# A two-layer hybrid generator on one core: the latent's GDN solution moved beside its RWKV scan, 84 instead of 64 expert slots placed first, and latent projections ahead of the context's later queries

## The chip, the cores and the metric

The kernel runs on 1 core of one Trainium2 chip. The metric is the device time of one execution in microseconds (us), lower is better. Three executions of the kernel before took 3139.51, 3136.21 and 3149.08 us, a median of 3139.51 us.

## The reference, cut to what matters

There are two layers over 256 latent tokens and 256 context tokens, width 1024, float32. Layer 0 mixes each stream by two bidirectional recurrences side by side (a chunked gated DeltaNet, "GDN", and RWKV-7), projects out, and runs PEER, a product-key expert layer. The latent stream starts from the final recurrence states of the context. Layer 1 needs the context only as keys and values of its attention.

```python
def even_layer(x_ctx, x_lat, ...):
    y_ctx, ctx_states = even_mixer(pre(x_ctx, ...) @ w_in, zeros, **mix)
    y_lat, _ = even_mixer(pre(x_lat, ...) @ w_in, ctx_states, **mix)
    x_lat = ffn_residual(x_lat + ml[2] * (y_lat @ w_out), ...)   # PEER
    x_ctx = ffn_residual(x_ctx + mc[2] * (y_ctx @ w_out), ...)   # PEER

def gdn_chunk_scan(q, k, v, g, beta, s0):          # chunks of 64
    lower = I + strict_lower((k*beta) @ k.T * decay)
    u, w = solve_triangular(lower, [v*beta, k*beta*exp(G)])
    # then 4 steps over the chunks, each needing the state of the last

def peer(h, wq, k1, k2, u, v):
    # per token, 8 heads: top 16 of 128 keys, twice; top 16 of the 256 pairs
    act = gelu(sum(u[eid] * h)); out = sum(gate * act * v[eid])
```

PEER reads, for each token, 8 x 16 rows of u and of v at computed indices.

## The kernel before, in words

**Slots.** A PEER tile is 128 tokens. Its 128 (head, rank) pairs are 128 slots of `experts` (L1263). A slot gathers one 2048-wide row of `peer_uv` per token (1 MB) by an indirect DMA that POOL issues (L1278), forms the dot product on DVE (L1281), the gelu and a diagonal matrix `di` on ACT and DVE (L1287 to L1291), and adds the v row into two PSUM banks by two 128x512 matmuls (L1293). Six buffers `g8` hold gathered rows, so about six gathers run ahead. There are six tiles: context 1 and 2, latent 1 and 2 in layer 0, and two in layer 1, 768 slots in all. Context tile 2 is cut: its first `CUT` = 64 slots (L152, L1785) stand directly behind context tile 1, the other 64 stand in layer 1 (L1806), beside the Hyena convolution.

**Picks.** Before a slot can be gathered its indices must be known. `peer_prep` (L1109) runs queries and scores for two heads at a time; `pick` (L1229) finds the top 16 on DVE, and its last row (L1253) writes the indices `ei` that the gathers of 32 slots read. The scores of tile 2 are kept and picked after those of tile 1.

**The latent mixer.** `rwkv_prep` (L721) projects and builds blocks, `solve` (L586) inverts triangular blocks (30 pairs of DVE operations in `solve1`, with a trip through DRAM ahead, `dn`, and one behind, `yd`, L619 and L632 to L634), `gdn_prep` (L428) projects q, k, v, and then computes the decays and the blocks N; `rwkv_scan` (L867) has four steps, `gates` (L959) four projections, `gdn_scan` (L664) four steps. Then come `rwkv_out`, `gdn_out`, `out_proj` and the latent's `peer_prep`.

**What sets the order.** `whole` (L1662) writes everything in one program, with Python generators that yield between pieces: `some(g, n)` takes n pieces, `mix(a, b, na, nb)` alternates, and a string of letters orders pieces (`h` is one of the context's query pieces, `l` one of the latent's RWKV preparation, `P` the latent's normalised input). The order of writing is the priority. The framework's scheduler then fixes a static order for each engine, in which slots written later fill the places that earlier work leaves free. Engines execute their order strictly, and so does SP, whose queue issues the plain loads and stores.

```python
for w in "hPhhlhllllll": ...                       # L1758
X = self.solve((lat.N,))
g = self.gdn_prep(lat)
some(g, 6)                                         # L1769, six projections
mix(g, self.rwkv_scan(lat, X, room2, "gm", False), 1, 1)
self.gates(lat)
X = self.solve((lat.N, True))                      # L1772, GDN
self.rwkv_out(lat)
g = self.gdn_scan(lat, X, pool=False)
```

Of the kernel before, what the change touches and what calls it, by code (L numbers as in the profile page):

```python
# [13 lines left out]
AF = mybir.ActivationFunctionType  # L14
# [136 lines left out]
PBUFS = dict(gm=3, sc=3, pv=2)  # L151
CUT = 64  # L152


class Net:
# [271 lines left out]

    def gdn_prep(self, s, tag="t2", ptag="gm", ntag="N", wtag="w"):  # L428

# [13 lines left out]
        nc.sync.dma_start(x, abd[0:2].rearrange("r c h s -> (r c h) s"))  # L443
        nc.sync.dma_start(bs, abd[2:4].rearrange("r c h s -> (r c h) s"))

        s.qkT = self.t("qkT", [128, 4, 4, 128])
# [28 lines left out]
        self.dump("vtok", s.vtok)  # L475

        nc.vector.tensor_scalar(x, x, C["dtb"], None, op0=ALU.add)
        ea = self.t("sy", [64, 65])
        e = ea[:, :64]
        nc.vector.scalar_tensor_tensor(e, x, -1.0, x, op0=ALU.mult, op1=ALU.min)  # L480
        nc.vector.tensor_copy(ea[:, 64:], C["alog"])
        self.exp(ea, [64, 65])
        z, z2, q = (self.t("sy", [64, 64]) for _ in J(3))
        nc.vector.tensor_scalar(z, e, 2.0, None, op0=ALU.add)
        nc.vector.reciprocal(z, z)
        nc.vector.tensor_mul(z, z, e)
        nc.vector.tensor_mul(z2, z, z)
        nc.vector.tensor_scalar(q, z2, 1.0 / 17, None, op0=ALU.mult)
        for m in (15, 13, 11, 9, 7, 5, 3):
            nc.vector.scalar_tensor_tensor(q, q, 1.0 / m, z2, op0=ALU.add, op1=ALU.mult)  # L490
        nc.vector.scalar_tensor_tensor(q, q, 1.0, z, op0=ALU.add, op1=ALU.mult)
        nc.vector.tensor_scalar(x, x, 0.0, None, op0=ALU.max)
        nc.vector.scalar_tensor_tensor(x, q, 2.0, x, op0=ALU.mult, op1=ALU.add)
        g = self.t("sy", [64, 64])
        nc.vector.tensor_scalar(g, x, ea[:, 64:65], -1.0, op0=ALU.mult, op1=ALU.mult)
        self.dump("g", g)
        fs = self.t("fs", [64, 5, 64])
        G = fs[:, 4]
        inn, off = self.t("sy", [64, 64]), self.t("off", [64, 4])
        ones3 = C["scan16"][:, 1:4]  # L500
        nc.vector.memset(off, 0.0)
        nc.vector.tensor_tensor_scan(inn[0:32], C["scan16"][0:32], g[0:32], 0.0, op0=ALU.mult, op1=ALU.add)
        nc.vector.tensor_tensor_scan(inn[32:64, ::-1], C["scan16"][32:64, ::-1], g[32:64, ::-1], 0.0,
                                     op0=ALU.mult, op1=ALU.add)
        nc.vector.tensor_tensor_scan(off[0:32, 1:4], ones3[0:32], inn[0:32, 15:63:16], 0.0, op0=ALU.mult, op1=ALU.add)
        nc.vector.tensor_tensor_scan(off[32:64, 2::-1], ones3[32:64], inn[32:64, 48:0:-16], 0.0,
                                     op0=ALU.mult, op1=ALU.add)
        nc.vector.tensor_tensor(G.rearrange("p (b s) -> p b s", b=4), inn.rearrange("p (b s) -> p b s", b=4),
                                off[:, :, None].to_broadcast([64, 4, 16]), op=ALU.add)
        self.dump("G", G)  # L510
        gend, gl = self.t("gend", [64, 1]), self.t("gl", [64, 1])
        nc.vector.tensor_copy(gend[0:32], G[0:32, 63:64])
        nc.vector.tensor_copy(gend[32:64], G[32:64, 0:1])
        nc.scalar.activation(fs[:, 2], bs, AF.Sigmoid)
        nc.scalar.activation(fs[:, 0], G, AF.Exp)
        nc.scalar.activation(fs[:, 1], G, AF.Exp, scale=-1.0, bias=gend)
        nc.scalar.activation(gl, gend, AF.Exp)
        nc.vector.tensor_mul(fs[:, 3], fs[:, 2], fs[:, 0])
        gbd = self.d("gbd", [2, 64, 64])
        nc.sync.dma_start(gbd[0], G)  # L520
        nc.sync.dma_start(gbd[1], fs[:, 2])
        yield

# [1138 lines left out]
    def whole(self, out):  # L1662
        nc, tc, A = self.nc, self.tc, self.A
        with ExitStack() as es:
# [13 lines left out]
            def some(g, n):  # L1678
                for _ in range(n):
                    next(g, 0)  # L1680

            def mix(a, b, na=1, nb=1, end=True):

                while True:
                    for _ in range(na):
                        if next(a, 0) == 0:
                            return rest(b) if end else None
                    some(b, nb)
# [68 lines left out]

            for w in "hPhhlhllllll":  # L1758
                if w == "P":
                    lat.hT = pre("l0_", [row(A["x"], i) for i in range(2)], 0)  # L1760
                    g = self.rwkv_prep(lat)
                else:
                    some(gp if w == "h" else g, 1)
# [3 lines left out]
            X = self.solve((lat.N,))  # L1767
            g = self.gdn_prep(lat)
            some(g, 6)  # L1769
            mix(g, self.rwkv_scan(lat, X, room2, "gm", False), 1, 1)  # L1770
            self.gates(lat)
            X = self.solve((lat.N, True))  # L1772
            self.rwkv_out(lat)
            g = self.gdn_scan(lat, X, pool=False)
            some(g, 3)
# [87 lines left out]
```

## Time and profile before

| what | value |
|---|---|
| three runs, median (lowest to highest) | 3139.51 us (3136.21 to 3149.08) |
| the profiled execution's own time | 3161.81 us |
| its span | 3159.9 us |
| PE, DVE, ACT, POOL busy, share of the span | 82%, 62%, 44%, 35% |
| DMA, mean rate over the span | 323 GB/s |

The profiled execution is 22.3 us above the median. The profile gives, for each engine, how long it was busy; a wait is named by what released it. In a table of windows each line is a stretch of the span, with the busy time of each engine and its number of instructions in brackets, then the mean clock granted to TensorE (1.00 is 2.4 GHz), the mean busy share of the 16 DMA engines, and what they moved. A slot appears in the trace as four matmul records.

### The profile page before, as it was taken

What the parts mean: (1) busy time and instruction counts of PE and PEld (TensorE: products, weight loads), DVE (VectorE), ACT (ScalarE), POOL (GpSimd) and SP (SyncE); (2) the same over time, 40 slices, a digit from 0 to 9 for tenths busy, and PEclk for the clock granted to TensorE, in tenths of its full rate; (3) what the DMA queues carried; (4) which work ended last, traced back from release to release, by engine and by line L of the source; (5) the groups of instructions that cost most, each with busy time, mean ns of one, the idle gap of its engine ahead of it and who ended that gap; (6) DMA issues with size and microseconds to landing.
All of it is one profiled execution on the core that took longest, in us unless ns stands there. A gap on an engine that the chain in (4) does not pass through costs nothing.

```text
span 3159.9 us, 40234 instructions
## 1 busy us (share of the span) xinstructions
PE 2584.2 (82%) x12216; PEld 1452.8 (46%) x12216; DVE 1955.8 (62%) x5457; ACT 1384.4 (44%) x3947; POOL 1116.7 (35%) x834
## 2 busy tenths in 40 slices
PE   6987978998888987669698777779986987778776
PEld 4765755655454544546243322226564554323222
DVE  2566456786966566358975555555647776655555
ACT  1331113455455545234455555554432543555554
POOL 0001202233332331022446377743302342556774
PEclk8996888999999998889899999999988999999999
DMA  9665658999898995389889999999966898999997
GB/s 316 228 203 158 197 165 321 340 347 349 330 323 322 352 357 184 104 317 328 315 339 421 393 420 420 417 398 347 354 219 253 307 389 322 383 388 421 421 421 327
DMA packets 296222, 1020.52 MB, mean 323 GB/s; under 512 B 64383, under 2 KB 167104, under 8 KB 197704
## 3 DMA queue, kind: packets, MB, share of 16 engines
q0 software_dynamic: 110592, 805.36, 64.6%
q1 hardware_dynamic: 185416, 212.60, 20.8%
q8 instruction: 99, 1.62, 0.2%
q14 instruction: 115, 0.94, 0.1%
HBM read 995.62 MB, written 22.25 MB: 322 GB/s over the span
## 4 chain that ended last, share of the span: by engine, by line
PE 38%; DMA 18%; POOL 14%; DVE 13%; issue 13%; ACT 3%; SPq 1%; POOLq 0%; DVEq 0%; ACTq 0%
PE pv L1293 14%; POOL g L1278 13%; DMA g<-in_l_peer_uv_dram,ei 7%; PE gm L269 4%; DVE g L1281 4%; PE gm L1142 3%; PE gm L1622 2%; DMA t<-in_l_mod_w_dram 2%; DMA w<-in_l_w_in_dram 1%; PE sc L269 1%; DMA w<-in_l_peer_wq_dram 1%; DMA g<-in_l_mod_w_dram 1%; PE pv L356 1%; POOL h L1278 1%; DMA qkT<-in_l_peer_wq_dram 1%
## 5 line engine op out<-in xcount | busy, mean ns | idle before, releaser
L1293 PE MATMUL pv<-g,di 128*128 128x512 f32 x2872 | 1427.6, 627 | 288.0 <-ACT di L1291 287.5
L1278 POOL DMA_INDIRECT g<-in_l_peer_uv_dram,ei x718 | 975.2, 1358 | 1576.5 <-PE pv L1293 712.6
L1293 PEld LDWEIGHTS pv<-g,di 128*128 128x128 f32 x2872 | 518.5, 195 | 1020.7 <-ACT di L1291 594.8
L1281 DVE SCALAR_TENSOR_TENSOR g<-g,h 128x1024 f32<-128x1024 f32 x352 | 429.6, 1221 | 179.2 <-DMA g<-in_l_peer_uv_dram,ei 178.5
L1287 ACT ACTIVATE gz<-act 128x1 f32<-128x1 f32 x768 | 154.2, 201 | 776.5 <-DVE g L1281 726.0
L1290 ACT ACTIVATE gz<-gz,gx 128x1 f32<-128x1 f32 x768 | 296.0, 386 | 108.4 <-DVE gx L1289 85.0
L1291 ACT ACTIVATE di<-c_ident,gz 128x128 f32<-128x128 f32 x768 | 307.4, 401 | 46.9 <-PE pv L1293 25.5
L1288 ACT ACTIVATE gz<-gz,act 128x1 f32<-128x1 f32 x768 | 296.3, 386 | 23.9
L1281 DVE SCALAR_TENSOR_TENSOR g<-g,vtok 128x1024 f32<-128x1024 f32 x128 | 156.8, 1225 | 128.0 <-DMA g<-in_l_peer_uv_dram,ei 128.0
L1281 DVE SCALAR_TENSOR_TENSOR g<-g,yv 128x1024 f32<-128x1024 f32 x128 | 156.0, 1219 | 60.4 <-DMA g<-in_l_peer_uv_dram,ei 60.4
L269 PE MATMUL gm<-h,w 128*128 128x256 f32 x752 | 178.5, 384 | 6.1 <-DMA w<-in_l_w_in_dram 6.0
L1289 DVE TENSOR_TENSOR gx<-act,gate 128x1 f32<-128x1 f32 x768 | 126.5, 165 | 69.3 <-ACT gz L1290 16.5
L1281 DVE SCALAR_TENSOR_TENSOR g<-g,ktok 128x1024 f32<-128x1024 f32 x110 | 134.0, 1219 | 54.1 <-DMA g<-in_l_peer_uv_dram,ei 52.5
L269 PEld LDWEIGHTS gm<-h,w 128*128 128x128 f32 x752 | 142.7, 193 | 47.7 <-issue 23.5
L1214 DVE MAX8 v<-t 128x8 f32<-128x128 f32 x64 | 15.5, 284 | 123.9 <-ACT t L1157 65.2
L1293 PE MATMUL pv<-h,di 128*128 128x512 f32 x136 | 68.2, 625 | 17.9 <-ACT di L1291 17.9
L1278 POOL DMA_INDIRECT h<-in_l_peer_uv_dram,ei x34 | 53.8, 1581 | 47.3 <-PE pv L1293 21.5
L1622 PE MATMUL gm<-og,w 128*128 128x128 f32 x384 | 51.4, 292 | 20.3 <-DMA w<-in_l_peer_wq_dram 20.3
L636 POOL MEMSET XT<- 32x512 f32 x4 | 2.1, 516 | 175.0 <-PE sc L269 174.8
L1622 PEld LDWEIGHTS gm<-og,w 128*128 128x128 f32 x384 | 50.1, 207 | 28.7 <-DMA w<-in_l_peer_wq_dram 20.5
L356 PE MATMUL pv<-t,scond 128*32 128x256 f32 x384 | 40.6, 511 | 23.4 <-DMA t<-in_l_mod_w_dram 21.7
L277 PE MATMUL gm<-w,h 128*128 128x256 f32 x192 | 48.9, 404 | 9.8 <-DMA w<-in_l_w_in_dram 9.8
(696 smaller groups left out, 3366.2 us busy)
## 6 DMA issues: line engine op xcount, KB each, us to landing
w<-in_l_w_in_dram SPq DMA_DIRECT2D x70, 512.0 KB
g<-in_l_mod_w_dram SPq DMA_DIRECT2D x24, 1024.0 KB
t<-in_l_mod_w_dram SPq DMA_DIRECT2D x48, 512.0 KB
w<-in_l_peer_wq_dram SPq DMA_DIRECT2D x26, 512.0 KB
g<-in_l_peer_uv_dram,ei POOLq DMA_INDIRECT x718, 9.5
qkT<-in_l_peer_wq_dram SPq DMA_DIRECT2D x9, 1024.0 KB
XT<-in_l_peer_wq_dram SPq DMA_DIRECT2D x14, 512.0 KB
XT<-in_l_w_in_dram SPq DMA_DIRECT2D x10, 512.0 KB
```

Of the source, the lines that this page charges most:

```text
L269: self.nc.tensor.matmul(ps[:, m], lhsT=wt[q][:, k, m * 128:(m + 1) * 128], rhs=hk, start=q == 0 and m == 0 and k == 0, stop=q == 1 and m = ...
L356: nc.tensor.matmul(ps[32 * j:32 * j + 32, :], lhsT=self.scond[:, k0 + k, :], rhs=w[:, k, j * 256:(j + 1) * 256], start=k0 + k == 0, stop=k ...
L1142: nc.tensor.matmul(pq[:, m], lhsT=w[1][k // 4][:, k % 4, m * 128:(m + 1) * 128], rhs=hT[i][:, k], start=k == 0, stop=k == KC - 1)
L1278: nc.gpsimd.indirect_dma_start(out=uv, out_offset=None, in_=A[l + "peer_uv"], in_offset=bass.IndirectOffsetOnAxis(ap=p.ei[n // 16][:, n % ...
L1281: ins = nc.vector.scalar_tensor_tensor(uv[:, :D], uv[:, :D], RT2PI, h, op0=ALU.mult, op1=ALU.mult, accum_out=x)
L1287: nc.scalar.activation(z[:, 0:1], x, AF.Square, scale=math.sqrt(0.044715) / RT2PI)
L1288: nc.scalar.activation(z[:, 0:1], z[:, 0:1], AF.Tanh, scale=x, bias=x)
L1289: nc.vector.tensor_mul(xg, x, gate[:, n:n + 1])
L1290: nc.scalar.activation(z[:, 1:2], z[:, 0:1], AF.Identity, scale=xg, bias=xg)
L1291: nc.scalar.activation(di, self.ident, AF.Copy, scale=z[:, 1:2])
L1293: nc.tensor.matmul(pv[hf], lhsT=di, rhs=uv[:, D + hf * 512:D + (hf + 1) * 512], start=n == ns[0], stop=n == ns[-1])
L1622: nc.tensor.matmul(pq[:, m], lhsT=wt[k // 4][:, k % 4, m * 128:(m + 1) * 128], rhs=hT[:, k], start=k == 0, stop=k == KC - 1)
```

## The change

The change writes the same operations in another order and moves one boundary. `CUT` becomes 84. The letters for the start of the latent become `hPlllhllllhlhlllh`: three latent projections stand ahead of the context's second pair of heads, and four pieces ahead of the third. `gdn_prep` gets `early=True`, which puts its decays ahead of its projections (the block of code moves into a function `decays`, unchanged). `gates` moves ahead of the RWKV scan. The scan is alternated with the two block pieces of `gdn_prep`, and its other two steps with the GDN solution, twelve pairs of DVE operations to a step.

```diff
-CUT = 64
+CUT = 84
...
-    def gdn_prep(self, s, tag="t2", ptag="gm", ntag="N", wtag="w"):
+    def gdn_prep(self, s, tag="t2", ptag="gm", ntag="N", wtag="w", early=False):
...
+        if early:
+            decays()
+            yield
...
+        if not early:
+            decays()
+            yield
...
-            for w in "hPhhlhllllll":
+            for w in "hPlllhllllhlhlllh":
...
             X = self.solve((lat.N,))
-            g = self.gdn_prep(lat)
-            some(g, 6)
-            mix(g, self.rwkv_scan(lat, X, room2, "gm", False), 1, 1)
+            g = self.gdn_prep(lat, early=True)
+            some(g, 7)
             self.gates(lat)
-            X = self.solve((lat.N, True))
+            gs = self.rwkv_scan(lat, X, room2, "gm", False)
+            mix(g, gs, 1, 1, False)
+            X = [None]
+            mix(self.solve1(X, 0, lat.N, True), gs, 12, 1)
             self.rwkv_out(lat)
-            g = self.gdn_scan(lat, X, pool=False)
+            g = self.gdn_scan(lat, X[0], pool=False)
```

In the rows below, lines of the changed kernel are 11 higher behind `gdn_prep` (L1293 becomes L1304, L619 becomes L630).

**Place 1, PE, the first step of the latent's GDN scan.** `sc<-S,qkT`, `sc<-s,h`, `sc<-s,s` and `sc<-s,AT` are the scan's products, `pv` the two matmuls of a slot. Before:

```order
L684 MATMUL sc_6997<-S_67_288,qkT_5471 64x128 x8
L684 MATMUL sc_6998<-S_67_288,qkT_5471 64x128 x8
L691 MATMUL sc_7019<-s_1140_7015,h_1111_6737 64x64 x16
L707 MATMUL sc_7046<-s_1141_7016,s_1137_6980 64x64 x8
L707 MATMUL sc_7057<-s_1141_7016,s_1137_6980 64x64 x8
L713 MATMUL sc_7068<-s_1141_7016,AT_6094 64x64
```

Now:

```order
L695 MATMUL sc_6997<-S_67_288,qkT_5535 64x128 x8
L695 MATMUL sc_6998<-S_67_288,qkT_5535 64x128 x8
L1304 MATMUL pv_10046<-g_2158_10906,di_10911 128x512
L1304 MATMUL pv_10047<-g_2158_10906,di_10911 128x512
L702 MATMUL sc_7019<-s_1140_7015,h_1111_6737 64x64 x16
L1304 MATMUL pv_10046<-g_2162_10919,di_10924 128x512
L1304 MATMUL pv_10047<-g_2162_10919,di_10924 128x512
L718 MATMUL sc_7046<-s_1141_7016,s_1137_6980 64x64 x8
L718 MATMUL sc_7057<-s_1141_7016,s_1137_6980 64x64 x8
L724 MATMUL sc_7068<-s_1141_7016,AT_5938 64x64
```

Before, all 192 early slots stand ahead of the scan and it has none inside. Now slot 191 stands ahead of the solution's first matmuls, three stand in the solution and 18 inside the four steps; the output projection follows behind slot 212.

**Place 2, SP, between the GDN solution's store and its loads.** `yddg` is the trip through DRAM behind the solution; `gd` and `zd` are stores of `gates`. Before:

```order
L619 DMA yddg_6662<-dg_6671 128x1024
L258 DMA XT_7662<-in_l_peer_wq_dram 128x4x256
L258 DMA XT_7664<-in_l_peer_wq_dram 128x4x256
L258 DMA w_6603<-in_l_w_in_dram 128x4x256
L258 DMA w_7503<-in_l_w_out_dram 128x4x256
L258 DMA w_7505<-in_l_w_out_dram 128x4x256
L379 DMA t_1216_7607<-l_mod_131 128x1024
L186 DMA S_3237_14486<-in_IFs_dram 128x512
L978 DMA gd_6606<-t_1102_6632 128x512
L973 DMA zd_6605<-t_1100_6626 128x512
L633 DMA h_1111_6737<-yddg_6662 32x16x32 x3
```

Now:

```order
L630 DMA yddg_6404<-dg_6413 128x1024
L186 DMA s_1119_6898<-in_ln_w_dram 128x512
L186 DMA s_1120_6900<-in_ln_b_dram 128x512
L993 DMA s_1121_6902<-gd_5838 64x512 x2
L258 DMA XT_7662<-in_l_peer_wq_dram 128x4x256
L258 DMA XT_7664<-in_l_peer_wq_dram 128x4x256
L643 DMA t_1112_6738<-yddg_6404 32x16x32
L644 DMA h_1111_6737<-yddg_6404 32x16x32
```

The weights of `gates` and `out_proj` and the stores `gd` and `zd` have left the place between store and loads.

**Place 3, DVE, the pick of heads 2 and 3 of context tile 1.** `g,act<-g,h` is a slot's dot product; `eid` and the cast to `ei` end the pick. Now, between the dot products of slots 32 and 33:

```order
L1292 SCALAR_TENSOR_TENSOR g_1501_8774,act_8368<-g_1501_8774,h_1373_8366 128x1024
L1229 MAX_INDEX pos_4215<-best_4214,t_708_4216 128x8 x2
L1268 TENSOR_TENSOR gate_3646<-best_4214 128x32
...
L1257 TENSOR_TENSOR t_711_4233<-pf_4229,c_iota_69_292 128x1024
...
L1259 TENSOR_TENSOR t_711_4233<-t_711_4233,i16f_4212 128x1024
...
L1261 TENSOR_REDUCE eid_4236<-t_711_4233 128x64
...
L1264 CAST ei_4239<-ef_3645 128x32
...
L1292 SCALAR_TENSOR_TENSOR g_1505_8787,act_8368<-g_1505_8787,h_1373_8366 128x1024
```

Before, the same pick ends behind the dot product of slot 20 or so, a dozen slots ahead of the first slot that needs it; now its last row stands behind slot 32, and slot 33 is the first that needs it. The pick of heads 4 and 5 stands at slot 30 before and at 58 now (needed by 65), that of heads 6 and 7 at 44 and 74 (needed by 97).

## Rows read from the trace of the kernel before

**Rows 1.** The page: span, granted clock and DMA share in 40 slices.

```profile
span 3159.9 us, 40234 instructions
...
PEclk8996888999999998889899999999988999999999
DMA  9665658999898995389889999999966898999997
```

**Rows 2.** The page: costliest groups (busy, mean ns, idle before), and DMA issues.

```profile
L1293 PE MATMUL pv<-g,di 128*128 128x512 f32 x2872 | 1427.6, 627 | 288.0 <-ACT di L1291 287.5
L1278 POOL DMA_INDIRECT g<-in_l_peer_uv_dram,ei x718 | 975.2, 1358 | 1576.5 <-PE pv L1293 712.6
...
g<-in_l_peer_uv_dram,ei POOLq DMA_INDIRECT x718, 9.5
```

**Rows 3.** Windows: PE, PEld, DVE, ACT, POOL busy; clock, DMA share, GB/s.

```profile
480.00:1217.00 737.00, 635.34 (x3181) 386.47 (x3180) 513.72 (x1516) 364.33 (x1018) 230.54 (x202) 0.94 0.92 339
1217.00:1274.00 57.00, 44.98 (x790) 32.52 (x790) 38.25 (x87) 38.68 (x135) 0.00 (x0) 0.83 0.37 115
1274.00:1345.00 71.00, 45.88 (x224) 39.21 (x222) 24.56 (x93) 10.60 (x33) 0.00 (x0) 0.84 0.26 82
...
2253.00:2314.00 61.00, 61.00 (x198) 35.34 (x197) 36.53 (x80) 27.47 (x80) 15.19 (x15) 1.00 0.98 377
2314.00:2400.00 86.00, 66.16 (x368) 55.22 (x367) 38.73 (x138) 22.34 (x62) 1.33 (x2) 0.86 0.36 117
```

**Rows 4.** Windows, the same columns: one stretch with slots alone.

```profile
2880.00:2960.00 80.00, 63.26 (x129) 21.55 (x128) 44.37 (x97) 44.10 (x128) 59.02 (x33) 1.00 1.01 421
```

**Rows 5.** Windows, the same columns: around the GDN solution's matmuls.

```profile
1172.00:1217.00 45.00, 22.16 (x92) 12.23 (x92) 24.26 (x54) 15.83 (x44) 11.35 (x12) 0.80 0.98 346
...
1238.00:1274.00 36.00, 26.55 (x514) 24.45 (x515) 23.68 (x51) 26.30 (x89) 0.00 (x0) 0.86 0.32 103
```

**Rows 6.** Groups of PE from 2253 to 2314 us: busy, mean ns, idle.

```profile
L1293 PE MATMUL pv<-g,di 128*128 128x512 f32 x78 | 36.1, 592 | 0.0
L277 PE MATMUL gm<-w,h 128*128 128x256 f32 x64 | 15.1, 379 | 0.0
L277 PE MATMUL sc<-w,h 128*128 128x256 f32 x16 | 4.0, 386 | 0.0
L1423 PE MATMUL sc<-t,S 128*128 128x512 f32 x8 | 3.9, 592 | 0.0
L1423 PE MATMUL sc<-t,AT 128*128 128x512 f32 x8 | 3.9, 592 | 0.0
L1406 PE MATMUL sc<-dg,AT 128*128 128x512 f32 x4 | 1.9, 592 | 0.0
L1458 PE MATMUL gm<-c_ident,ktok 128*128 128x128 f32 x8 | 1.4, 272 | 0.0
```

**Rows 7.** SP's queue in order of time: start, us, line.

```profile
1156.87 0.33 SPq L619 DMA_DIRECT2D yddg<-dg  x1
...
1163.42 17.33 SPq L258 DMA_DIRECT2D w<-in_l_w_out_dram  x2
...
1190.39 0.33 SPq L978 DMA_DIRECT2D gd<-t  x1
...
1191.29 1.64 SPq L633 DMA_DIRECT2D h<-yddg  x3
```

**Rows 8.** DVE in order of time, end of the second pick.

```profile
556.68 0.09 DVE L1218 MATCH_VALUE_LOAD pos<-best,t 128x8 f32 x1
...
563.27 1.20 DVE L1281 SCALAR_TENSOR_TENSOR g<-g,h 128x1024 f32<-128x1024 f32 x1
...
566.05 1.21 DVE L1281 SCALAR_TENSOR_TENSOR g<-g,h 128x1024 f32<-128x1024 f32 x1
...
568.35 0.16 DVE L1253 CAST ei<-ef 128x32 int32<-128x32 f32 x1
```

**Rows 9.** Windows of line L1278 alone (gathers issued, clock, DMA share, GB/s).

```profile
1200.00:1240.00 40.00, 3.74 (x3) 0.79 0.68 234
...
1320.00:1360.00 40.00, 7.10 (x7) 0.65 0.35 131
```

More of the change, by code (lines that the diff above doesn't have):

```diff
@@ L444, in gdn_prep, with decays @@
         nc.sync.dma_start(bs, abd[2:4].rearrange("r c h s -> (r c h) s"))
+        loc = {}
+        def decays():
+            nc.vector.tensor_scalar(x, x, C["dtb"], None, op0=ALU.add)
+            ea = self.t("sy", [64, 65])
+            e = ea[:, :64]
+            nc.vector.scalar_tensor_tensor(e, x, -1.0, x, op0=ALU.mult, op1=ALU.min)
+            nc.vector.tensor_copy(ea[:, 64:], C["alog"])
+            self.exp(ea, [64, 65])
+            z, z2, q = (self.t("sy", [64, 64]) for _ in J(3))
+            nc.vector.tensor_scalar(z, e, 2.0, None, op0=ALU.add)
+            nc.vector.reciprocal(z, z)
+            nc.vector.tensor_mul(z, z, e)
+            nc.vector.tensor_mul(z2, z, z)
+            nc.vector.tensor_scalar(q, z2, 1.0 / 17, None, op0=ALU.mult)
+            for m in (15, 13, 11, 9, 7, 5, 3):
+                nc.vector.scalar_tensor_tensor(q, q, 1.0 / m, z2, op0=ALU.add, op1=ALU.mult)
+            nc.vector.scalar_tensor_tensor(q, q, 1.0, z, op0=ALU.add, op1=ALU.mult)
+            nc.vector.tensor_scalar(x, x, 0.0, None, op0=ALU.max)
+            nc.vector.scalar_tensor_tensor(x, q, 2.0, x, op0=ALU.mult, op1=ALU.add)
+            g = self.t("sy", [64, 64])
+            nc.vector.tensor_scalar(g, x, ea[:, 64:65], -1.0, op0=ALU.mult, op1=ALU.mult)
+            self.dump("g", g)
+            fs = self.t("fs", [64, 5, 64])
+            G = fs[:, 4]
+            inn, off = self.t("sy", [64, 64]), self.t("off", [64, 4])
+            ones3 = C["scan16"][:, 1:4]
+            nc.vector.memset(off, 0.0)
+            nc.vector.tensor_tensor_scan(inn[0:32], C["scan16"][0:32], g[0:32], 0.0, op0=ALU.mult, op1=ALU.add)
+            nc.vector.tensor_tensor_scan(inn[32:64, ::-1], C["scan16"][32:64, ::-1], g[32:64, ::-1], 0.0,
+                                         op0=ALU.mult, op1=ALU.add)
+            nc.vector.tensor_tensor_scan(off[0:32, 1:4], ones3[0:32], inn[0:32, 15:63:16], 0.0, op0=ALU.mult, op1=ALU.add)
+            nc.vector.tensor_tensor_scan(off[32:64, 2::-1], ones3[32:64], inn[32:64, 48:0:-16], 0.0,
+                                         op0=ALU.mult, op1=ALU.add)
+            nc.vector.tensor_tensor(G.rearrange("p (b s) -> p b s", b=4), inn.rearrange("p (b s) -> p b s", b=4),
+                                    off[:, :, None].to_broadcast([64, 4, 16]), op=ALU.add)
+            self.dump("G", G)
+            gend, gl = self.t("gend", [64, 1]), self.t("gl", [64, 1])
+            nc.vector.tensor_copy(gend[0:32], G[0:32, 63:64])
+            nc.vector.tensor_copy(gend[32:64], G[32:64, 0:1])
+            nc.scalar.activation(fs[:, 2], bs, AF.Sigmoid)
+            nc.scalar.activation(fs[:, 0], G, AF.Exp)
+            nc.scalar.activation(fs[:, 1], G, AF.Exp, scale=-1.0, bias=gend)
+            nc.scalar.activation(gl, gend, AF.Exp)
+            nc.vector.tensor_mul(fs[:, 3], fs[:, 2], fs[:, 0])
+            gbd = self.d("gbd", [2, 64, 64])
+            nc.sync.dma_start(gbd[0], G)
+            nc.sync.dma_start(gbd[1], fs[:, 2])
+            loc.update(fs=fs, gl=gl, gbd=gbd)
@@ L475, in gdn_prep @@
         self.dump("vtok", s.vtok)
[L477 to L519, printed above, removed]
@@ L520, in gdn_prep @@
-        nc.sync.dma_start(gbd[0], G)
-        nc.sync.dma_start(gbd[1], fs[:, 2])
-        yield
+        if not early:
+            decays()
+            yield
+        fs, gl, gbd = loc["fs"], loc["gl"], loc["gbd"]
         ft = self.t(tag, [64, 320])
```

## The prediction

> **What bounds the kernel now.** I read the page's 40 slices first, to see where the kernel is short of something. DMA is the busiest resource of the whole span, and the slices show two holes in it, 5 and 3 tenths around 1200 to 1360 us and 3 around 2320 to 2400 us [rows 1]. Next come the costliest groups: the slots' matmuls are the largest load of PE, and the idle time ahead of them ended mostly with `di`, the last link of a chain that begins with a gather [rows 2]. Where slots run alone, 33 gathers pass in 80 us, 2.42 us each, at a DMA share of 1.01, and PE needs 63.26 / 33 = 1.92 us for one [rows 4]. So a slot costs 2.42 us of DMA or 1.92 us of PE, whichever the stretch is short of.
>
> Then I read windows by stage. From 480 to 1217 us PE is busy 635 of 737 us and the DMA share is 0.92: the latent's mixer and 192 slots fill this stage together. From 1217 us the slots are used up: 57 us with the GDN solution's matmuls and the scan at a DMA share of 0.37, then 71 us with the output projection and the latent's queries at 0.26 [rows 3]. Between 1200 and 1240 us three gathers are issued, and the next seven after 1320 us [rows 9]. From 2253 to 2314 us, in layer 1, it is the other way round: PE is busy 61.0 of 61 us at clock 1.00 [rows 3]. The change takes slots from the second place and puts them in the first.
>
> **The change part by part.** No operation is added or removed. There are four terms.
>
> *A, layer 1.* The 64 slots beside the Hyena convolution become 44. Their order among themselves and around them is the old one, shifted by 20, so the last 20 fall away. The stretch of the last 20 slots is 2253 to 2314 us: 78 matmul records are 19.5 slots [rows 6]. PE is what is short there, so the stretch shrinks to the rest of PE's work. The other groups sum to 15.1 + 4.0 + 3.9 + 3.9 + 1.9 + 1.4 = 30.2 us [rows 6]. Some waits that slots cover today come out: I give them 3 us. 61 - 30 - 3 = 28, so **A = -28 us**. The best case is all 36.1 us of the slots' matmuls [rows 6]; the worst leaves 20 us, if 11 us of waits come out in place of 3. The chain of tile 2's last residual, norm and keys starts earlier by the same amount and is not late next; the queries' matmuls are.
>
> *B, the GDN scan.* 20 more slots stand beside the GDN solution's matmuls and scan, 18 of them inside the scan's steps, one at each point where PE hands over to DVE or ACT. The scan alone has PE busy 26.55 of 36 us, so 9.5 us are free [rows 5]. 20 slots bring 20 x 1.92 = 38.4 us of PE; less the 9.5 us this lengthens the stretch by 29 us. Against this, the stretch now runs at a clock of 0.86 and a stretch with slots at 1.00 [rows 5, 4]: PE's own 26.55 us would become 26.55 x 0.86 = 22.8, 4 us less, and three of the slots fall into the solution's waits, some 5 us. **B = +20 us**. DMA is no obstacle: 20 x 2.42 = 48.4 us fit in 57 + 20 us. The least is 0 (the 20 slots vanish in 57 us with a DMA share of 0.37, 36 us free, and in waits ahead of them), the most 48 (gathers in series with the chain).
>
> *C, the wait for the solution's trip through DRAM.* The store of the solution is issued at 1156.87 us, and the first load back at 1191.29, because SP, in order, first waits with two loads of the output projection (17.33 us) and then for `gates` to finish its store (1190.39) [rows 7]. Both are gone from there (place 2). From 1172 to 1217 us PE is busy 22.16 of 45 us [rows 5]. Free are thus at most 22.8 us of PE, and 34 us of the trip. But the same row has DMA at a share of 0.98: the loads moved away have to be done earlier, in a stage at 0.92. I take **C = -20 us**, close to the PE figure because that row is the stretch itself; the ends are 0 and -34. `gates`' four projections and their weights now pass between the projections and the scan; they are the same loads, and PE had waits there already.
>
> *D, the second pick.* In the new order the indices of slots 33 to 64 are ready only behind slot 32's dot product (place 3). Before, the piece from 556.68 to 568.35 us is this work with two dot products inside: 11.7 - 2 x 1.2 = 9 us [rows 8]. Then come the gather's issue, 1.36 us, and its landing, 9.5 us after issue [rows 2]. For about 20 us no slot can start; PE has some latent blocks to do, and the DMA engines the latent's weights. **D = +10 us**, half; the ends are 0 and 20. The later picks keep a margin of 6 slots or more. The early decays are small DVE operations on 64 partitions, the same ones as before; DVE is busy 514 of 737 us in the stage [rows 3] and hides them, and without that cover they would cost a few us.
>
> The sum is -28 + 20 - 20 + 10 = -18 us. The profiled execution took 3161.8 us, 22.3 above the median of the runs; from it the sum gives 3143.8, and from the median, which the new runs will be set against, 3139.5 - 18 = **3121.5 us**, 0.57% less. About 0.5%, 15.7 us, is what a measurement of this kernel can tell from no change.
>
> **The rivals.**
>
> *The slots only change places (about +2 us, 3141.5).* If the stage before 1217 us is held by its DMA, C is 0: every byte that was waited for is still to be moved. Then -28 + 20 + 0 + 10 = +2. For it speaks the 0.98 of [rows 5] in the very stretch that C counts on; against it, that PE stands idle half of this stretch, which in the stage is the exception. The Trainium skill, DMA: Bandwidth & Descriptors, Issuing engines are not separate DMA queues, says that transfers started by SP and by POOL run on the same engines and interleave, which speaks for this case; the row's 0.98 agrees with it, and by that rule the sum is +2 rather than -18.
>
> *Layer 1's end loses its clock (+10 us, 3149.5).* Without slots PE has gaps, and the clock falls: from 2314 to 2400 us, with no slots, it is 0.86, against 1.00 just before [rows 3]. If all of the 30 us of work left fell from the upper level, 2.4 GHz, to 1.2 GHz, it would take 60 and A would be near 0: 0 + 20 - 20 + 10 = +10. Against it: PE is at work in 66 of those 86 us and loses only 0.14 of its clock, and the work left is dense. The Trainium skill, TensorE: Matmul & The Clock Gate, The HAM clock gate, holds that the slow state is the default and activity lifts it; the falls in [rows 3] agree in direction, and by the rule taken fully the sum is +10.
>
> *Slower: gathers ahead of the chain (+30 us, 3169.5).* PE executes its static order strictly. In the scan a slot stands ahead of each hand-over (place 1), and if its gather has not landed, the scan's next product waits behind it. Were the gathers in series with the scan, B would be 20 x 2.42 = 48 us, and the solution's small loads would queue behind them, so that C is 0: -28 + 48 + 0 + 10 = +30. It decides from B + C = 34 on. For it speaks that slots wait on the gather's chain for 288 us in all [rows 2]; against it, that six buffers run ahead and that DMA is two thirds free here.
>
> **How the numbers follow.** My forecast gets 0.48, the first rival 0.29, the clock 0.08, the third 0.15. Faster by over 0.5% is thus 0.48, within 0.5% 0.37, slower 0.15. The forecast's own range, by the ends of A to D taken two at a time, is 3085 to 3140. For 8 in 10 it reaches up to the first two rivals and a part of the third: 3085 to 3155.
>
> **What would show it.** A: the stretch from the end of layer 1's 44 slots to the first keys of the context is some 33 us, with PE nearly full. B: gathers are issued until after 1260 us, and the scan's first to last product takes about 56 us in place of 36. C: the first `yddg` load is issued within 10 us of its store, and PE is idle under 10 us ahead of the solution's matmuls. D: a gap of gathers of 10 to 20 us behind slot 32. The prediction is wrong if slot 191 comes later than 1217 us by more than D, if the scan takes over 75 us, or if the layer 1 stretch stays above 45 us.

## The result, and the profile after

The changed kernel takes **3166.26 us**, the median of 6 runs (3159.77 to 3176.67); the kernel before, run beside it, 3139.52 (6 runs, 3130.95 to 3149.08). The ratio is 1.0073, with a 95% interval of 1.0054 to 1.0092: 27 us slower, where 18 us less was forecast, and 11 us above the end of the range.

The page's slices after, beside [rows 1]: the first hole in the DMA share, 5 and 3 tenths in the 16th and 17th slice, is now 6 and 5 in the 17th and 18th, so it is filled in part and stands later; the second, 6 and 6 in the 30th and 31st, is deeper, 4 and 5, since layer 1 has 20 slots fewer there.

```profile
PEclk8996888999899998988899999999998999999999
...
DMA  9665658899899898658899999999845899999997
```

The costliest group as in [rows 2]. The idle time ahead of the slots' matmuls has grown by 12 us, from 288.0 to 300.1:

```profile
L1304 PE MATMUL pv<-g,di 128*128 128x512 f32 x2872 | 1427.8, 626 | 300.1 <-ACT di L1302 294.1
```

A single execution can lie 20 us off its kernel's median, and most of the 22 us by which the execution of before shown ahead does so lies behind 2400 us. I therefore cut the program into stretches at events that every trace has, and count from the first slot's dot product: the last triangular operation of the GDN solution on DVE, the solution's last matmul on PE, the scan's last product, the dot products of the first and last latent slot, and of the first and last slot of layer 1's own tiles. "Before" is here a second execution of the kernel before (`e1_before_again`, 3143.62 us). Its stretches and those of the execution shown ahead agree within 4 us, except the last, where they are 17 us apart (723.9 and 740.7). All are us:

| stretch | before | changed | difference | forecast |
|---|---|---|---|---|
| first slot to last triangular operation | 660.9 | 691.0 | +30.1 | (D) +10 |
| to the solution's last matmul | 83.1 | 65.0 | -18.1 | (C) -20 |
| to the scan's last product | 34.6 | 65.3 | +30.7 | (B) +20 |
| to the first latent slot | 78.0 | 77.7 | -0.3 | 0 |
| latent tiles, first to last slot | 743.2 | 740.4 | -2.8 | 0 |
| to the first slot of layer 1's tiles | 312.7 | 284.6 | -28.1 | (A) -28 |
| to the last slot | 723.9 | 728.0 | +4.1 | 0 |

The sum is +15.7, in single executions; the medians say +27 (the changed kernel's execution is 5 us below its median, that of before 4 us above the 3139.52). The first two rows belong together, since one event parts them: the solution as a whole comes 12 us later instead of 10 earlier.

*The scan.* Windows with the columns of [rows 3]. After, the first line runs from the last triangular operation to the solution's end, and the second from there to the scan's end:

```profile
1185.00:1250.00 65.00, 42.79 (x459) 22.16 (x458) 39.28 (x92) 30.38 (x96) 15.77 (x15) 0.84 0.91 308
1250.00:1315.00 65.00, 59.67 (x584) 34.97 (x582) 43.71 (x100) 46.29 (x158) 12.99 (x13) 0.95 0.81 289
```

Before, from the solution's end to the scan's end:

```profile
1235.00:1270.00 35.00, 25.91 (x523) 23.61 (x522) 24.26 (x52) 26.30 (x89) 0.00 (x0) 0.90 0.31 105
```

And PE's groups in the 65 us of the scan, after; the last line is the first group of products before:

```profile
L1304 PE MATMUL pv<-g,di 128*128 128x512 f32 x72 | 36.3, 638 | 2.5 <-ACT di L1302 2.2 <-issue 0.3
L695 PE MATMUL sc<-S,qkT 128*64 128x128 f32 x128 | 10.8, 280 | 0.0
L702 PE MATMUL sc<-s,h 64*64 64x64 f32 x128 | 5.9, 243 | 2.7 <-DVE nr L216 2.2 <-DVE s L698 0.5
...
L684 PE MATMUL sc<-S,qkT 128*64 128x128 f32 x128 | 11.4, 279 | 0.4 <-DVE S L709 0.4
```

72 records are 18 slots and 36.3 us, 2.0 us each. The scan's own work on PE is then 59.67 - 36.3 = 23.4 us and PE's idle time 5.3; before, 0.6 us of 25.91 belong to a slot, 25.3 are the scan's own and 9.1 idle. So 35.7 us of slots came in, 1.9 us of the scan's own busy time went, at a clock of 0.95 in place of 0.90, and 3.8 of idle were filled: +30. That the clock took the 1.9 us is not shown: a product of the first group takes 280 ns, and took 279.

*The solution's trip.* SP's queue after (columns as in [rows 7]). The first load stands 13.2 us behind its store, in place of 34 [rows 7], not within the 10 that were hoped for: the load ahead of it waits until 1200.29 for the RWKV scan to free an `XT` buffer. The ten small loads themselves take until 1231 us:

```profile
1188.11 0.33 SPq L630 DMA_DIRECT2D yddg<-dg  x1
...
1200.29 0.94 SPq L258 DMA_DIRECT2D XT<-in_l_peer_wq_dram  x2
1201.33 2.65 SPq L643 DMA_DIRECT2D t<-yddg  x1
1204.03 10.22 SPq L644 DMA_DIRECT2D h<-yddg  x1
1214.30 7.33 SPq L643 DMA_DIRECT2D t<-yddg  x1
1221.67 4.05 SPq L644 DMA_DIRECT2D h<-yddg  x1
...
1230.89 0.49 SPq L645 DMA_DIRECT2D t<-yddg  x1
```

And PE, in order, waits 11.30 us for the transposes of the first of them, longer than any single wait for `di` in this stage (10.2 us), and then 4.28 us more for the rest:

```profile
1231.63 0.23 PE L657 MATMUL sc<-h,N 32*32 32x32 f32 x1 [11.30 <-DVE h L649]
...
1236.23 0.26 PE L657 MATMUL sc<-h,N 32*32 32x32 f32 x1 [4.28 <-DVE h L649]
```

The store itself is 31 us later than in [rows 7] (1156.87 there): the triangular operations end late. The line of the last one, after, and then of the second execution of before:

```profile
1184.60 0.19 DVE L625 TENSOR_TENSOR dg<-dg,kTh 128x30 f32<-128x30 f32 x1
```

```profile
1152.23 0.19 DVE L614 TENSOR_TENSOR dg<-dg,kTh 128x30 f32<-128x30 f32 x1
```

*The second pick.* The gap of gathers behind slot 32 is there, 22.5 us on POOL:

```profile
625.00 0.94 POOL L1289 DMA_INDIRECT g<-in_l_peer_uv_dram,ei  x1 [22.52 <-issue]
```

Counted from the first slot, slot 64 is 15 us late by it (245.4 against 230.0 us) and slot 81 is not late at all (301.0 against 301.7).

### The profile page after: what moved, and what is told of

It reads as the page before. It is cut to its first block, busy times and chain, and to the rows that moved or that the text cites. A ratio compares the mean times of both kernels' runs of the same rounds, so it can differ in the third digit from the quotient of the medians.

```text
span 3159.6 us, 40185 instructions
## 1 busy us (share of the span) xinstructions
PE 2582.6 (82%) x12216; PEld 1443.3 (46%) x12216; DVE 1949.9 (62%) x5457; ACT 1382.9 (44%) x3947; POOL 1126.7 (36%) x834
## 3 DMA queue, kind: packets, MB, share of 16 engines
q1 hardware_dynamic: 185416, 212.60, 20.8%
## 5 line engine op out<-in xcount | busy, mean ns | idle before, releaser
L1304 PE MATMUL pv<-g,di 128*128 128x512 f32 x2872 | 1427.8, 626 | 300.1 <-ACT di L1302 294.1
L1289 POOL DMA_INDIRECT g<-in_l_peer_uv_dram,ei x718 | 985.1, 1372 | 1576.2 <-PE pv L1304 755.0
L1304 PEld LDWEIGHTS pv<-g,di 128*128 128x128 f32 x2872 | 515.8, 195 | 1035.2 <-ACT di L1302 607.5
L1304 PE MATMUL pv<-h,di 128*128 128x512 f32 x136 | 68.2, 625 | 18.4 <-ACT di L1302 18.4
L1225 DVE MAX8 v<-t 128x8 f32<-128x128 f32 x64 | 15.6, 285 | 107.0 <-ACT t L1168 56.1
L1289 POOL DMA_INDIRECT h<-in_l_peer_uv_dram,ei x34 | 53.2, 1565 | 43.0 <-PE pv L1304 28.1
L1304 PEld LDWEIGHTS pv<-h,di 128*128 128x128 f32 x136 | 23.8, 191 | 56.8 <-ACT di L1302 36.9
```

The source lines that it names most:

```text
L1289: nc.gpsimd.indirect_dma_start(out=uv, out_offset=None, in_=A[l + "peer_uv"], in_offset=bass.IndirectOffsetOnAxis(ap=p.ei[n // 16][:, n % ...
L1304: nc.tensor.matmul(pv[hf], lhsT=di, rhs=uv[:, D + hf * 512:D + (hf + 1) * 512], start=n == ns[0], stop=n == ns[-1])
```

## The experiments

Times are medians; each ratio is to the kernel before on the same chip, with its 95% interval. The stretches are those of the table above.

**The kernel before, once more**, as the trace to set the others against.

> The kernel before, profiled once more, because its first profile stands 22 us above its own median. If that excess sits in stages which the change does not touch (layer 1's tiles, behind 2400 us), theory A (the change lengthens the chain up to the first latent slot by 38 us and gains 25 us in layer 1) needs another 10 to 15 us of loss, which should show as a shorter stretch before 1217 us here. If the excess sits ahead of the first latent slot, that slot's dot product comes some 15 us earlier here than 1355 us.

3143.62 us in its one run, where the kernel before's 29 others beside it have a median of 3141.24. Its stretches stand in the table. The expectation had two places for the 22 us, and most are in the first: of the 18 us between the two traces' spans, 17 lie in layer 1's own tiles, and the first latent slot comes 7 us earlier, not 15.

**Which part costs: the order, the slots, the letters.** Three kernels with a part undone each:

```diff
# e2_order_cut64, on the changed kernel
-CUT = 84
+CUT = 64
# e3_cut84_alone, on the kernel before
-CUT = 64
+CUT = 84
# e4_old_letters, on the changed kernel
-            for w in "hPlllhllllhlhlllh":
+            for w in "hPhhlhllllll":
```

> The new order with the old boundary of 64 slots. Theory A, the order costs (the latent's chain reaches the end of the GDN solution later, 1249.8 against 1238.0 us in the two traces, and the 20 slots are about neutral): +10 to +25 us against the kernel before. Theory B, the slots cost (20 slots in the scan cost more than layer 1 gives back, the order is worth nothing either way): within 6 us of the kernel before. My forecast's term C, were it right and hidden by B: 10 to 20 us faster.

> The old order with 84 slots first. Its scan holds the slots 192 to 212, as the changed kernel's does. Theory A: the 20 slots cost 29 us in the scan and give back 25 us or more in layer 1, so within 8 us of the kernel before, or a little faster. Theory B: +18 to +30 us. My forecast's sum without C and D: -28 + 20 = -8 us.

> The changed kernel with the old string of letters, so without the late second pick of context tile 1. Theory A with the pick as its cause (a gap of 15.7 us in the gathers behind slot 32): 10 to 15 us faster than the changed kernel, +12 to +17 us against the kernel before. If the gap is made up later in the stage (slot 80 has the same time in both traces): no more than 4 us from the changed kernel, so +23 to +30 us.

Then the two kernels that are missing from the square: the mixer's order alone (e4's edit and e2's), and the letters alone on the kernel before.

> The change without its 84 slots (64 stay) and without its row of letters (the old row stays): what is left is the early decays, the gates' projections moved, and the GDN solution beside the RWKV scan. Theory 'the stage is full' (the wait for the solution's trip through DRAM is filled already, so C is worth 0): the solution's matmuls end 740 to 748 us behind the first slot's dot product, as before (743), and the time is within 6 us of the kernel before. Theory 'C is there and something else hid it' (the 20 slots or the letters): the solution's matmuls end at least 12 us earlier relative to the first slot, and the time is 8 to 20 us below the kernel before.

> The kernel before with the new row of letters alone, 64 slots. Theory 'D is a delay that the stage makes up': a gap of 15 to 25 us of gathers behind slot 32, made up by slot 80 or so, and the time within 5 us of the kernel before. Theory 'the late pick costs for good' (the queries that the letters push back end up behind the scan or in it): 6 to 15 us over the kernel before, with the first latent slot that much later.

| kernel | time | ratio (interval) | solution's end | scan | first latent slot | latent's last to layer 1's first |
|---|---|---|---|---|---|---|
| before (e1) | 3143.62 | - | 744.0 | 34.6 | 856.6 | 312.7 |
| changed | 3166.26 | 1.0073 (1.0054 to 1.0092) | 756.0 | 65.3 | 899.1 | 284.6 |
| e2, order and letters | 3147.76 | 1.0027 (1.0009 to 1.0045) | 744.4 | 35.1 | 856.5 | 314.8 |
| e3, 84 slots | 3156.52 | 1.0049 (1.0027 to 1.0071) | 748.0 | 70.6 | 894.7 | 287.4 |
| e4, order and 84 slots | 3148.84 | 1.0021 (1.0000 to 1.0043) | 745.7 | 67.5 | 887.8 | 284.9 |
| e5, order | 3135.05 | 0.9980 (0.9964 to 0.9996) | 736.3 | 35.7 | 849.8 | 313.5 |
| e6, letters | 3148.21 | 1.0021 (1.0003 to 1.0039) | 744.8 | 35.4 | 857.4 | 315.3 |

The stretches are again those of single executions, and the ones of e2 and e5 were the slowest of their 12 (3167.45 and 3145.09 us, 20 and 10 above their medians); 14 and 10 us lie in layer 1's own tiles (738.0 and 733.4 us against 723.9), behind the stretches of this table.

What follows. The 20 slots cost the scan 31.8 us (e5 to e4), 36.0 (before to e3) or 30.2 (e2 to the changed kernel), and put off the solution ahead of it by 4 to 12; all in all the first latent slot comes 38 to 43 us later. Layer 1 gives 25 to 30 back. By the medians they cost 14 to 19 us. Neither "order costs" (e2 at +10 to +25, e3 within 8) nor "slots cost" (e2 within 6, e3 at +18 to +30) holds: e2 is at +6.5, e3 at +15. The order without the letters is the one part that gains: 7.4 us, with the solution 7.7 us earlier, between the two theories of e5, and at the edge of what can be told from nothing. The letters cost: 6 us alone, 13 in the new order (e5 to e2), 17 with the slots as well (e4 to the changed kernel). If the pick was the cause, e4 was expected 10 to 15 below the changed kernel and 12 to 17 above the kernel before; it is 17 below and 8 above.

The gap of gathers is made up (slot 81), so they must cost elsewhere. The latent's RWKV scan has its first product 473.5 us behind the first slot before and at 497.2 with the letters alone, at 508.0 with the order and at 538.9 with both (e2), and with the 84 slots at 510.8 (e4) and 534.8 (the changed kernel): the letters delay the latent's own chain by 24 to 31 us, where two executions of one kernel differ by 7. The triangular operations of the GDN solution end 14 to 23 us later with them (17 in the old order). In the old order the solution itself does not feel it (744.0 to 744.8): 83 us lay between the two, and now 67 do. In the new order that distance is only 64 to 69 us, and a part comes through: the solution ends 8.1 us later (e5 to e2) and 10.3 (e4 to the changed kernel), the first latent slot 6.7 and 11.3. The other 6 us of each cost, and all 6 of e6, whose first latent slot is 0.8 us late, were not placed.

**SP's place alone.** In the changed kernel the latent's odd heads use the even head's weights, so that no load of a weight stands ahead of the small loads. Four loads of 0.5 MB are left out, and with them a part of the computation:

```diff
-                if h % 2:
+                if h % 2 and not cond:
+                    wt = ws[0][1]
+                elif h % 2:
```

> The changed kernel, but the latent's odd heads of queries use the weights of the even head beside them: their weight loads (0.5 MB each, four of them) are left out, among them the one that stands ahead of the solution's small loads in SP's order and waits for the RWKV scan to free its tile. Part of the computation is changed by this. Theory 'the wait on SP was only replaced' (by the wait for that tile): the first of the small loads is issued within 4 us of the solution's store (13 in the changed kernel), and the solution's matmuls end 744 to 748 us behind the first slot's dot product in place of 756. Theory 'the DMA engines are full': the small loads are issued earlier and take as much longer, and the matmuls end 752 us or more behind the first slot. Both expect the scan to keep its 65 us. The end of the kernel may come up to 12 us earlier for the loads left out alone, and says nothing.

3173.86 us in its one run, which says nothing of the change. The first small load is 8.1 us behind its store, not within 4: SP now waits, until 1200.37 us, with the load of `gd`, which is next in line. The solution ends at 755.4 against 756.0 us. But the last triangular operation comes 5.5 us later in this execution (696.5 against 691.0), and from there the solution takes 58.9 us in place of 65.0. So SP's place may be worth some 6 us of the trip; one execution can't settle it, since two of one kernel differ by up to 4 us in such a stretch. PE begins the solution 6 us earlier, its waits there get shorter (15.6 us for L657 in the changed kernel), and the ten loads take 26.3 us from the first issue to the last, in place of 29.6:

```profile
PE sc L657 <- DVE h L649: 5.7, 2, 3.7
...
PE sc L658 <- DMA t<-yddg: 3.0, 1, 3.0
```

Of the theory "the DMA engines are full" the late end came, 755.4 us, but the loads issued earlier did not take as much longer. They passed beside gathers at a DMA share of 1.05 (1202 to 1229 us).

**Fewer slots ahead of the solution.** The kernel before with `CUT = 44`, and e5 with `CUT = 44`:

> The kernel before with 44 slots of context tile 2 ahead of the latent in place of 64; 84 wait for layer 1 in place of 64. Theory 'throughput' (the stage from the first slot to the GDN scan is bounded by its slots, and nothing is gained by putting slots beside it): 20 slots fewer end it 35 to 48 us earlier, layer 1 gets 36 to 48 us longer, and the time is within 10 us of the kernel before. Theory 'the mixer's chain bounds the stage, and slots fill its gaps': the stage ends less than 15 us earlier, and the time is 20 to 40 us over the kernel before.

> The new order of the mixer with the old letters, and 44 slots in place of 84 ahead of the latent: to be set against the kernel before with 44 slots, whose GDN solution ended 687.3 us behind the first slot's dot product and whose scan ended 38.6 us later. In both all slots are used up before the solution's matmuls, so the stage is emptier than with 64. Theory 'the stage is full' (C is small only because slots fill the wait): here the solution ends 15 us or more earlier than 687.3. Theory 'the new order moves the triangular steps back as much as it removes from the wait': it ends 0 to 10 us earlier, as with 64 slots (7).

e8 takes 3168.65 us, 1.0105 (1.0083 to 1.0126); e9 3169.36 in its one run. The covered stage behaves as "throughput" says, and more: the first latent slot comes 52 us earlier (804.4 against 856.6), 2.6 us for each slot, above the 2.42 of a gather [rows 4]. But layer 1 pays 67 us (379.7 against 312.7), 3.4 for each slot, so that the time is where the other theory put it. 64 is a kink: the next 20 slots bring only 28 there. Why these 20 cost layer 1 more than a gather's 2.42 us each was not traced.

Most of the 52 us lies in the solution. From the last triangular operation to its last matmul it takes 83.1 us with 64 slots, and 35.1 with 44, where next to none is left to stand in between; with the new order 64.2 (e5) and 28.1 (e9). PE's slots in these stretches, before and in e8:

```profile
L1293 PE MATMUL pv<-g,di 128*128 128x512 f32 x76 | 39.7, 652 | 7.2 <-ACT di L1291 7.2
...
L1293 PE MATMUL pv<-g,di 128*128 128x512 f32 x2 | 1.0, 592 | 0.0
```

Slots and the waits ahead of them take 46.9 of the 83 us, and 1.0 of the 35: PE executes them ahead of the solution in its static order. Their transfers go with them, though, and SP's waits with the transfers. The same two loads of the output projection, before and in e8:

```profile
1160.23 19.20 SPq L258 DMA_DIRECT2D w<-in_l_w_out_dram  x2
...
1150.78 1.84 SPq L258 DMA_DIRECT2D w<-in_l_w_out_dram  x2
```

The first small load stands 36 us behind its store before, and 16 in e8. So these runs do not part the slots' place on PE from their gathers beside the small loads; in the changed kernel both count, with 34 us of slots and waits for `di`, and 15.6 us of waits for the loads, in 65 us. The order's own gain is 1.7 us with 44 slots and 7.7 with 64: it ends the triangular operations later (657.5 against 652.1 us) by nearly as much as it takes from the trip. The second theory of e9's expectation holds. Behind the solution e9 loses its gain again: its scan takes 44.1 us against 38.6 in e8, and its first latent slot comes 4 us later (808.6 against 804.4).

**Slots where they do not stand ahead of the chain.** The changed kernel with the old letters, and the last slots of the early part held back behind the GDN scan:

```diff
+        late = ExitStack()
         for n in ns:
+            if cond and l == "l0_" and len(ns) == CUT and n == 64:
+                late.enter_context(self.tc.issue_after(self.last_p3))
...
+        late.close()
```

e11 is this with 84 slots; e10 has 64 and `n == 44`, e12 84 and `n == 44`.

> The changed kernel with the old letters and its 84 slots, but slots 65 to 84 may not be issued before the last product of the latent's GDN scan: they stand beside the output projection and the latent's queries, where PE is busy 45 of 71 us, and none inside the scan. Theory 'a slot costs 1.92 us of PE wherever it stands, less the idle time of the place': the scan is back to 35 us, the stretch behind it gets 12 to 38 us longer (20 x 1.92 = 38, less up to 26 of idle), the layer 1 stretch keeps its -28, and the time is between 3111 and 3141, most likely some 3125. Theory 'the chain there waits for slots too': the stretch gets 38 us longer or more, and the time is 3141 or above.

> The new order with the old letters and 64 slots of context tile 2, of which the last 20 may not be issued before the last product of the GDN scan: 44 ahead of the solution, 20 beside the output projection and the latent's queries. Theory 'slots that stand ahead of the solution in PE's order bound it': the solution's matmuls end some 685 us behind the first slot, as with 44 slots in all (736 with 64 ahead of it), the scan takes 35 to 41 us, the stretch from its end to the first latent slot's dot product 104 us as with 20 slots there (78 without): that dot product comes 12 to 20 us earlier than in the kernel before, and the time is 3122 to 3133. Theory 'the slots cost the same everywhere': it comes within 6 us of the kernel before's, and the time within 8 us of it.

> The same with 84 slots, 40 of them behind the scan. Theory 'what idle time there is behind the scan is used up by the first 20': the stretch gets 38 us longer again, 142 us, layer 1 28 us shorter, and the time is 8 to 12 us over the run with 64 slots split at 44. Theory 'there is room for more': the stretch is below 130 us, and the time below that run's.

| kernel | ahead + behind the scan | time | ratio (interval) | solution's end | scan | scan's end to first latent slot | first latent slot |
|---|---|---|---|---|---|---|---|
| e5 | 64 + 0 | 3135.05 | 0.9980 (0.9964 to 0.9996) | 736.3 | 35.7 | 77.8 | 849.8 |
| e11 | 64 + 20 | 3152.15 | 1.0029 (1.0006 to 1.0052) | 731.2 | 41.5 | 104.3 | 877.0 |
| e10 | 44 + 20 | 3138.19 | 0.9996 (0.9978 to 1.0014) | 692.7 | 43.5 | 101.9 | 838.1 |
| e12 | 44 + 40 | 3131.36 | 0.9966 (0.9948 to 0.9983) | 690.6 | 44.1 | 125.2 | 859.9 |

By their stretches e11 and e10 came out much as the first theory of each said: 20 slots behind the scan cost 24 to 27 us there instead of 32 inside it, and the solution ends 44 us earlier when 20 slots fewer stand ahead of it. In e12 the second theory holds: 20 more behind the scan cost only 23 (125.2 - 101.9), and the stretch stays below 130. Only the scan is longer than expected, 44 us. **e12 is faster than both kernels**, 9.5 us below the kernel before, with an interval clear of 1, and 35 below the changed one. In the times, e11 and e10 missed: 3152 and 3138 where 3111 to 3141 and 3122 to 3133 were expected. The profiled executions of these two took 3137.2 and 3127.7 us, the second shortest and the shortest of their 12 runs, and e12's was the shortest too (3116.27); what their other executions do differently was not seen. So e12's gain is the 9.5 us of the medians, not the 27 by which its profiled execution is ahead of e1's.

Three windows of e12, the stretch ahead of the scan, the scan, and the stretch behind it, and then the last two of e5:

```profile
1152.00:1181.00 29.00, 14.84 (x371) 13.24 (x373) 14.65 (x33) 7.34 (x20) 1.26 (x1) 0.56 0.55 164
1181.00:1226.00 45.00, 30.29 (x543) 28.10 (x534) 30.88 (x72) 32.55 (x114) 0.00 (x0) 0.77 0.26 83
1226.00:1343.00 117.00, 108.49 (x379) 63.30 (x378) 72.67 (x220) 54.29 (x168) 40.98 (x37) 0.99 0.94 366
```

```profile
1230.00:1266.00 36.00, 28.03 (x527) 24.64 (x520) 24.90 (x52) 26.41 (x89) 0.00 (x0) 0.91 0.31 102
1266.00:1337.00 71.00, 44.96 (x223) 38.25 (x221) 27.72 (x110) 9.32 (x32) 0.10 (x1) 0.83 0.26 83
```

Behind the scan e5 has PE idle 26 of 71 us at a clock of 0.83, and e12 8.5 of 117 at 0.99. The 40 slots cost 47 us there (125.2 - 77.8), 1.2 each, the cheapest place in this part of the program.

## Why the prediction was wrong, by its steps

By the stretches, A is on its mark, B missed by 11 us, and C and D, which were to bring the solution 10 us earlier and brought it 12 later, by 22. The step that failed is C; B is mis-sized.

**A, layer 1: right.** Forecast -28, measured -28.1 (-25.3 in e3, -28.6 from e5 to e4, -30.2 from e2 to the changed kernel). The mechanism held too: what PE has to do there beside the slots [rows 6] was forecast at 30 us of work and 3 of waits, and fills this window behind the last of the 44 slots:

```profile
2291.00:2324.00 33.00, 29.79 (x121) 20.58 (x119) 14.98 (x37) 4.25 (x12) 0.00 (x0) 1.00 0.37 115
```

The rival in which layer 1's end loses its clock would have left A near 0 and is out: the granted clock is 1.00. That price holds for these 20 slots only: the 20 before them bring 67 (e8).

**B, the slots beside the scan: mis-sized, +30.7 in place of +20.** The first part of the step, "20 x 1.92 = 38.4 us of PE; less the 9.5 us this lengthens the stretch by 29 us", is near what came, in part by luck: 18 of the 20 slots stand in the scan, at 2.0 us each, and they filled 3.8 us of idle time, not 9.5. The two credits behind it were wrong. The clock did rise to 0.95, but the scan's own work shrank by 1.9 us, not 4. The 5 us for slots that "fall into the solution's waits" brought nothing: the solution's last matmul came 12 us later, and PE still stood idle for 11.3 us in one of those waits.

**C, the wait for the trip through DRAM: wrong.** The step says "Free are thus at most 22.8 us of PE, and 34 us of the trip". It read the trip's length and took for granted that the store would be issued at its old time. The change deals the triangular operations out over the RWKV scan's last steps, and that scan now stands behind `gates`' projections; they end 11 us later by the order alone (672.1 against 660.9) and 30 later with the letters and slots. Which part of the order delays them was not tried alone. The trip did get 18 to 19 us shorter (83.1 to 65.0, and 64.2 in e5), the -20 of the forecast, and the later start took back 11 or 30. Both of the forecast's own tests failed narrowly: the first load came 13 us behind its store, not within 10, and PE was idle 11.3 us ahead of the solution, not under 10. SP's order, which the step took for the cause of the wait, is a part of it: with its place wholly free the trip may be some 6 us shorter still (e7), and with 20 slots fewer it is less than half as long (e8 and e9).

**D, the late pick: near in size, wrong in place.** Forecast +10 at the gathers; the gap came, 22.5 us, and was made up by slot 81. The letters cost 13 to 17 us in the new order, of which 7 to 11 show at the first latent slot, through the latent's own chain, which the step did not follow: with the letters the latent's RWKV scan starts 24 to 31 us later, the triangular operations end 14 to 23 later, and in the new order the solution has less time behind them to absorb it.

**The rivals.** "The slots only change places" had C at 0, and the solution was indeed not earlier, though not with an unchanged trip: the trip got 18 us shorter and started later. Its reason, that every byte waited for is still to be moved, is not shown: whether the loads that were moved ahead delay the start was not tried. Its B was too small as well. The Trainium skill, DMA: Bandwidth & Descriptors, Issuing engines are not separate DMA queues, which was cited for it, says that transfers started by SP and by POOL run on the same engines and interleave. The traces agree: SP's ten small loads take 13.1 us (e5) to 29.6 us (the changed kernel) from the first issue to the last beside POOL's gathers, and 5.8 where none pass (e9). "Gathers ahead of the chain" had the right sign and, at +30, the right size against the median's +27, which was luck: it had B at 48 and C at 0. Its mechanism is half of the truth: the chain does wait behind slots in PE's order, but in front of the solution rather than inside the scan, where PE was busy 92%, waited 2.2 us for `di`, and DMA had room (0.81). I gave it 0.15 because "six buffers run ahead and that DMA is two thirds free here"; that was read from the scan's row, and the chain's wait lay one stretch earlier, in the row with a DMA share of 0.98 [rows 5].

**The range.** It was too short by its own terms: with B and C at their upper ends the time is 3169.5 us, yet "taken two at a time" the ends were made to stop at 3140. A reading is wrong too, with nothing resting on it: the slices of [rows 1] show 6 tenths, not 3, around 2320 to 2400 us; the low share there is the 0.36 of [rows 3].

**What is left open.** By stretches the changed kernel's execution is 16 us longer than that of before, and the medians differ by 27. Runs of one kernel spread by 10 to 30 us, so the other 11 us, and the 6 us of the letters that no stretch shows, can't be placed. How much of the solution's trip belongs to the slots on PE, and how much to their transfers, stays open.

## What to carry to other kernels

When a wait is taken away, ask when the event ahead of it will now happen: dealing a serial chain out over another chain's steps shortens the wait and delays its start, and only the sum counts. On an engine with a static order, independent work that fills gaps was cheap behind a dependent chain where the engine is idle (1.2 to 1.3 us a slot here), near its full price beside the chain (1.5 to 1.8), and dearer than its own work when it stands ahead of the chain's next link (2.1 from e5 to e9, 2.6 from before to e8). The last price is near the pace of the gathers, 2.42; that they set it is not shown. Try the parts of a change one by one: here one part gained 7 us, another lost 6 to 17, and a better place for the slots was somewhere else.

## What the runs showed of the hardware

Work ahead of a chain shows in the granted clock of the chain. With slots right up to the solution (e5) PE is busy 20.8 of 29 us ahead of the scan at a granted clock of 0.76 (1201 to 1230 us), and the scan has 0.91 and takes 35.7 us. In e12, where PE is busy 14.8 of 29 us ahead of the scan and the granted clock is 0.56 there, between the levels of 1.2 and 2.4 GHz, the same scan has 0.77 and takes 44.1. Three of the scan's groups of matmuls, first in e12 and then in e5:

```profile
L695 PE MATMUL sc<-S,qkT 128*64 128x128 f32 x128 | 13.6, 325 | 0.4 <-DVE S L720 0.4
...
L702 PE MATMUL sc<-s,h 64*64 64x64 f32 x128 | 5.6, 244 | 8.4 <-DVE s L698 6.3 <-DVE nr L220 2.0
L718 PE MATMUL sc<-s,s 64*64 64x64 f32 x128 | 5.2, 271 | 6.0 <-ACT s L703 6.0
```

```profile
L695 PE MATMUL sc<-S,qkT 128*64 128x128 f32 x128 | 12.0, 279 | 0.4 <-DVE S L720 0.4
...
L702 PE MATMUL sc<-s,h 64*64 64x64 f32 x128 | 5.2, 237 | 3.4 <-DVE nr L220 2.0 <-DVE s L698 1.4
L718 PE MATMUL sc<-s,s 64*64 64x64 f32 x128 | 4.5, 248 | 4.2 <-ACT s L703 4.2
```

The clock has the smaller share of the 8 us: its four groups sum to 31.7 us in e12 and 28.0 in e5, while waits for DVE and ACT inside the scan are 14.7 us in e12 and 8.0 in e5, where DVE and ACT execute less other work beside it (x52 and x89 instructions in the window, against x72 and x114).

Small loads take longer to get away beside gathers. The ten small loads of the solution took 5.8 us from the first issue to the last where no gather passed (e9), and 13.1 (e5), 16.6 (e4), 26.3 (e7) and 29.6 us (the changed kernel) beside gathers, at DMA shares of 0.97 to 1.07.
